# Two attention mixers: the values' products of query tiles taken in pairs

## The chip, the cores and the metric

The kernel runs on one core of a Trainium2 chip. The core has a matrix engine (TensorE, PE in the profile; its loads of the stationary operand stand in rows of their own as PEld), a vector engine (VectorE, DVE), an engine for functions and copies (ScalarE, ACT), a general one (GpSimdE, POOL) and one that issues transfers (SyncE, SP). The metric is the time of one execution on the device in microseconds. Each engine runs its own instructions in the order of its queue and waits on semaphores for the others.

## The reference, cut to what matters

Two layers work on 512 latent tokens (a grid of 8 rows by 64 columns) and 256 context tokens, 1024 channels wide, everything in 32-bit floats. A layer has three mixers: a Fourier mix, a neighbourhood attention and a latent attention. Their results are gated, merged and projected, and a gated feed-forward part follows. The context tokens read context alone, and the second layer does not renew them. The change lies in the two attentions, each with 8 heads of 64 channels:

```python
def softmax_attend(q, k, v, scale):
    s = jnp.einsum('bqhd,bkhd->bhqk', q, k, preferred_element_type=jnp.float32) * scale
    p = jax.nn.softmax(s, axis=-1).astype(v.dtype)
    return jnp.einsum('bhqk,bkhd->bqhd', p, v)
```

The latent attention lets every latent query read all 768 keys, and a context query the 256 context keys. The neighbourhood attention lets a latent query read a clamped window of 8 x 16 grid positions, with a learned bias per offset, and all 256 context keys, under one softmax:

```python
s = jnp.concatenate([s_loc.reshape(b, h, GRID_W, n_loc), s_ctx], axis=-1)
p = jax.nn.softmax(s, axis=-1).astype(v.dtype)
...
return (jnp.einsum('bhwkj,bkwjhd->bwhd', p_loc, v_win)
        + jnp.einsum('bhwc,bchd->bwhd', p_ctx, v_ctx))
```

## The kernel before

A token tile is 128 tokens: tiles 0 to 3 are latent, 4 and 5 context. Layer 0 handles six query tiles in its attentions, layer 1 only the four latent ones. Heads go in four pairs. A **unit** is one query tile of one head pair in one mixer, made by `na_unit` (neighbourhood) or `mla_unit` (latent attention), so that there are (6 + 4) x 4 x 2 = 80 units in all. A unit has four parts:

- *scores*: the products of queries and keys for both heads into PSUM banks (lines 1163 to 1167, and `mm3` at line 269), the maximum on DVE, and the exponentials on ACT. These also leave the sums of a row's probabilities in the small tile `ac`. The unnormalized probabilities are the tiles `p` and `mp`.
- *norm*: `row_scale` adds the two sums of a row (line 1041), takes reciprocals (line 1043) and spreads them to the 64 channels of each head, as the tile `rw` (line 1045), on DVE.
- *transpose*: PE turns the probabilities by key chunks of 128 into PSUM (lines 1195, 1491 and 1496), and ACT and DVE copy them into `pT` or `mpT` (lines 1198, 1492 and 1498). `scale_rows` turns `rw` in the same way (line 1051) and copies it back (line 1052).
- *values*: per key chunk and head, one f32 product with 64 channels of the values as the stationary operand and the 128 queries of the transposed probabilities as the moving one (line 1210 in the neighbourhood attention, line 1506 in the latent one). The two heads of the pair write partitions 0 to 63 and 64 to 127 of one bank, in two column halves of the array (`tile_position`). DVE multiplies by the turned scales on the way out (lines 1213 and 1509), and the last unit of a head pair issues the store to DRAM.

A latent unit of the latent attention has 6 chunks of 128 keys, which are the same for all latent tiles. A latent unit of the neighbourhood attention has the two context chunks, which are the same for all tiles, and two chunks of its own window; for tiles 0 and 3 the last of these has 64 keys. A context unit has two context chunks in both.

`pipeline` writes down the order of the units: at step n the norm of unit n-1, the scores of unit n, the values of unit n-2, and then the transposes of unit n-1. Between these steps `weave` deals out filler steps (the projections of the next head pair, gates ahead of their turn, modulation blocks) by their costs, the numbers `c` of a unit among them. Then the framework's scheduler orders the instructions of each engine with a simulated timeline and adds the waits. Tiles come from pools: `bufs` says how many buffers stand behind a tag, and a new tile waits until all users of the old one in its buffer are through. PSUM has eight banks, which all parts share through `ps()`.

The product at line 532 of the modulation blocks appears in the prediction as well: a f32 product with 256 moving columns in four column strips of 32.

Of the kernel before, what the change touches and what calls it, by code (L numbers as in the profile page):

```python
# [9 lines left out]
F32 = mybir.dt.float32  # L10
# [5 lines left out]
P = 128  # L16
# [117 lines left out]
class Kern:  # L134
# [900 lines left out]
    def row_scale(self, pool, accs, n):  # L1035

        nc = self.nc
        s = accs[:, :, 0]
        if n == 2:
            s = self.t(self.sm, [P, 2], "ssum", F32, 6)  # L1040
            nc.vector.tensor_add(s, accs[:, :, 0], accs[:, :, 1])
        r = self.t(self.sm, [P, 2], "srec", F32, 6)
        nc.vector.reciprocal(r, s)
        w = self.t(pool, [P, P], "rw", F32, 2)
        nc.vector.tensor_copy(w.rearrange("p (a b) -> p a b", a=2), r.unsqueeze(2).to_broadcast([P, 2, 64]))
        return w

    def scale_rows(self, w):

        ps = self.ps()  # L1050
        self.nc.tensor.transpose(ps[:, :P], w, self.ident)
        self.nc.scalar.copy(w, ps[:, :P])
        return w

    def qk_steps(self, l, hp):
# [32 lines left out]
        return a + b  # L1088

    def pipeline(self, groups, fills, begin=()):  # L1090

# [31 lines left out]

    def na_unit(self, l, hp, i):

# [21 lines left out]
        def scores():  # L1147
# [9 lines left out]
            st["ys"], st["p"] = self.nys, []  # L1157
            st["ac"] = self.t(self.sm, [P, 2, 2], "ac", F32, 6)
            ss = []
# [9 lines left out]
            for j in range(2):  # L1169
                s = ss[j]  # L1170
                p = self.t("na", [P, 512], "p", F32, 4)
                nm = self.t(self.sm, [P, 1], "nm", F32, 6)
                ac = st["ac"][:, j]
# [10 lines left out]
                st["p"].append(p)  # L1184

        def norm():
            st["w"] = self.row_scale("na", st["ac"], 2 if lat else 1)

        def transpose():
            ch = chunks()  # L1190
            st["pT"] = []
            for j in range(2):
                pt = self.ps()
                for c, (col, r, v) in enumerate(ch):
                    nc.tensor.transpose(pt[:r, c * P:(c + 1) * P], st["p"][j][:, col:col + r], self.ident)
                pT = self.t("na", [P, 512], "pT", F32, 4)
                full = sum(P for _, r, _ in ch if r == P)
                nc.scalar.copy(pT[:, :full], pt[:, :full])
                if full < len(ch) * P:
                    nc.scalar.copy(pT[:64, full:full + P], pt[:64, full:full + P])  # L1200
                st["pT"].append(pT)
            st["r"] = self.scale_rows(st["w"])

        def values():
            ch = chunks()
            y = self.ps()
            for c, (col, r, v) in enumerate(ch):
                for j in range(2):
                    h = 2 * hp + j
                    nc.tensor.matmul(y[64 * j:64 * j + 64, :P], v[:r, h * DH:(h + 1) * DH],  # L1210
                                     st["pT"][j][:r, c * P:(c + 1) * P], start=c == 0, stop=c == len(ch) - 1,
                                     tile_position=(0, 64 * j))
            nc.vector.tensor_mul(st["ys"][:, i * P:(i + 1) * P], y[:, :P], st["r"])
            if i == (NT if cx else NTL) - 1:
                nc.scalar.dma_start(self.ybuf[1][hp * P:(hp + 1) * P, :tt], st["ys"][:, :tt])

        f = 1.0 if lat else 0.5
        return dict(scores=scores, norm=norm, transpose=transpose, values=values, c=(0.9 * f, 0.9 * f, 1.1 * f))

    def attention(self, l):  # L1220
# [14 lines left out]
        st += self.qk_steps(l, 0)  # L1235
        units = [[self.na_unit(l, hp, i) for i in range(nq)] for hp in range(4)]
        pl = on_pool if NA_POOL else list
# [99 lines left out]
    def mla_main(self, l, steps):  # L1337
# [91 lines left out]
        self.mq = {}  # L1429
        units = [[self.mla_unit(l, hp, i) for i in range(nq)] for hp in range(4)]  # L1430
        pl = on_pool if MLA_POOL else list
# [5 lines left out]

    def mla_unit(self, l, hp, i):
        nc = self.nc
# [8 lines left out]
        def scores():  # L1448
# [3 lines left out]
            st["ys"], st["p"] = self.mys, []  # L1452
            st["ac"] = self.t(self.sm, [P, 2, 2], "ac", F32, 6)
            qq = slice(i * P, (i + 1) * P)
# [11 lines left out]
            for j in range(2):  # L1466
                scj = sc[:, 256 * j:256 * j + 256]
                p = self.t("m3", [P, T], "mp", F32, 4)
                nm = self.t(self.sm, [P, 1], "nm", F32, 6)
                ac = st["ac"][:, j]  # L1470
                if lat:
# [7 lines left out]
                st["p"].append(p)  # L1479

        def norm():
            st["w"] = self.row_scale("m3", st["ac"], 2 if lat else 1)

        def transpose():
            pT = self.t("m3", [P, 2, NT, P], "mpT", F32, 2)
            st["pT"] = pT
            if lat:
                for j in range(2):
                    pt = self.ps()
                    for c in range(4):  # L1490
                        nc.tensor.transpose(pt[:, c * P:(c + 1) * P], st["p"][j][:, c * P:(c + 1) * P], self.ident)
                    nc.scalar.copy(pT[:, j, 0:4, :], pt.rearrange("p (a b) -> p a b", b=P))
            pt = self.ps()
            for j in range(2):
                for c in range(2):
                    nc.tensor.transpose(pt[:, (2 * j + c) * P:(2 * j + c + 1) * P],
                                        st["p"][j][:, (4 + c) * P:(5 + c) * P], self.ident)
            nc.vector.tensor_copy(pT[:, :, 4:6, :], pt.rearrange("p (a c b) -> p a c b", a=2, b=P))
            st["r"] = self.scale_rows(st["w"])

        def values():
            y = self.ps()
            for a, c in enumerate(cl):
                for j in range(2):
                    h = 2 * hp + j
                    nc.tensor.matmul(y[64 * j:64 * j + 64, :P], self.vm[:, c, h * DH:(h + 1) * DH],
                                     st["pT"][:, j, c, :], start=a == 0, stop=a == len(cl) - 1,
                                     tile_position=(0, 64 * j))
            nc.vector.tensor_mul(st["ys"][:, i * P:(i + 1) * P], y[:, :P], st["r"])
# [681 lines left out]
```

## Time and profile before

| | us |
|---|---|
| median of 3 runs | 2399.32 |
| lowest and highest run | 2399.12, 2402.32 |
| profiled execution | 2407.74 |
| its span on the core | 2405.9 |
| PE busy in the span | 2292.3 |
| DVE busy | 1361.3 |
| ACT busy | 1105.7 |
| POOL busy | 991.1 |

The profile comes from one execution. "Busy" counts the time in which an engine has at least one instruction in work; matmuls overlap each other, so that a long duration of one says little and the distance between the starts of two says more. In a row of the timeline, neighbours of one kind are merged: start, time to the end of the last one, engine, line, operation, output and inputs by their names in the program, stationary shape, moving shape, count, and in brackets the idle time before it with the instruction that ended it. A row of a group has the count, the busy time in us and the mean ns of one, and then the idle time before them and what ended it. A product of f32 operands stands in the profile as two loads and two matmuls.

### The profile page before, as it was taken

What the parts mean: (1) busy time and instruction counts of PE and PEld (TensorE: products, weight loads), DVE (VectorE), ACT (ScalarE), POOL (GpSimd) and SP (SyncE); (2) the same over time, 40 slices, a digit from 0 to 9 for tenths busy, and PEclk for the clock granted to TensorE, in tenths of its full rate; (3) what the DMA queues carried; (4) which work ended last, traced back from release to release, by engine and by line L of the source; (5) the groups of instructions that cost most, each with busy time, mean ns of one, the idle gap of its engine ahead of it and who ended that gap; (6) DMA issues with size and microseconds to landing.
All of it is one profiled execution on the core that took longest, in us unless ns stands there. A gap on an engine that the chain in (4) does not pass through costs nothing. (4 is left out here: it accounts for less than half of the span.)

```text
span 2405.9 us, 37733 instructions
## 1 busy us (share of the span) xinstructions
PE 2292.3 (95%) x14370; PEld 1992.7 (83%) x14370; DVE 1361.3 (57%) x2491; ACT 1105.7 (46%) x2472; POOL 991.1 (41%) x755
## 2 busy tenths in 40 slices
PE   6999999999999998999999999999999988999997
PEld 4877688878988787999988888788888867999875
DVE  7335456658435668555541352344668566888634
ACT  4335466644332253444442252565665424555532
POOL 2311143124238446334348343324403665423483
PEclk9999999999999998999999999999999999999998
DMA  9446421117665331222252243222214642333431
GB/s 340 141 147 234 174 77 61 38 59 258 235 245 183 110 122 49 97 105 97 70 216 77 80 145 114 78 69 90 86 44 171 211 149 103 113 106 106 140 114 62
DMA packets 105409, 307.80 MB, mean 128 GB/s; under 512 B 12070, under 2 KB 21228, under 8 KB 105228
## 3 DMA queue, kind: packets, MB, share of 16 engines
q1 hardware_dynamic: 86444, 261.48, 31.8%
q10 hardware_dynamic: 15552, 38.63, 4.2%
q0 software_dynamic: 3232, 5.28, 0.8%
q8 instruction: 113, 1.85, 0.3%
q14 instruction: 68, 0.56, 0.1%
HBM read 262.06 MB, written 47.48 MB: 129 GB/s over the span
## 5 line engine op out<-in xcount | busy, mean ns | idle before, releaser
L211 POOL TENSOR_TENSOR wlo<-raw,whi 128x512 fp32r<-128x512 f32 (+2 forms) x420 | 566.1, 1356 | 889.4 <-ACT whi L210 841.5
L210 ACT CAST whi<-raw 128x512 fp32r<-128x512 f32 (+1 forms) x447 | 273.6, 616 | 431.3 <-PE ps L1648 98.5
L509 PE MATMUL ps<-tp,whi 128*128 128x384 f32 (+1 forms) x1120 | 273.7, 315 | 2.2 <-POOL tp L444 1.0
L509 PE MATMUL ps<-AH,whi 128*128 128x384 f32 (+1 forms) x636 | 197.8, 314 | 3.9 <-DVE hx L490 1.5
L509 PEld LDWEIGHTS ps<-tp,whi 128*128 128x128 f32 x1120 | 194.7, 188 | 6.7 <-issue 2.9
L509 PE MATMUL ps<-AH,wlo 128*128 128x384 f32 (+1 forms) x636 | 197.3, 311 | 1.0 <-DVE wlo L211 1.0
L277 PE MATMUL ps<-AH,whi 128*128 128x512 f32 (+1 forms) x584 | 188.1, 368 | 10.0 <-ACT hx L1890 7.4
L509 PE MATMUL ps<-AL,whi 128*128 128x384 f32 (+1 forms) x636 | 196.2, 310 | 0.0
L277 PE MATMUL ps<-AL,whi 128*128 128x512 f32 (+1 forms) x584 | 183.3, 362 | 1.5 <-DVE AL L733 1.5
L277 PE MATMUL ps<-AH,wlo 128*128 128x512 f32 (+1 forms) x584 | 183.1, 361 | 0.0
L509 PE MATMUL ps<-tp,wlo 128*128 128x384 f32 (+1 forms) x560 | 175.2, 313 | 0.0
L2003 PE MATMUL ps<-whi,hx 128*128 128x512 f32 x520 | 165.2, 397 | 8.5 <-ACT hx L1995 5.0
L325 PE MATMUL ps<-wlo,AH 128*128 128x512 f32 (+1 forms) x352 | 134.2, 382 | 0.0
L325 PE MATMUL ps<-whi,AL 128*128 128x512 f32 (+1 forms) x352 | 133.9, 381 | 0.0
L325 PE MATMUL ps<-whi,AH 128*128 128x512 f32 (+1 forms) x352 | 132.4, 384 | 0.0
L277 PEld LDWEIGHTS ps<-AH,whi 128*128 128x128 f32 x584 | 101.7, 193 | 31.9 <-ACT hx L1890 7.9
L2003 PEld LDWEIGHTS ps<-whi,hx 128*128 128x128 f32 x520 | 97.8, 189 | 33.8 <-ACT hx L1995 5.6
L509 PEld LDWEIGHTS ps<-AH,whi 128*128 128x128 f32 x636 | 119.5, 188 | 7.2 <-DVE hx L490 2.1
L509 PEld LDWEIGHTS ps<-AH,wlo 128*128 128x128 f32 x636 | 119.7, 188 | 1.4 <-DVE wlo L211 1.2
L509 PEld LDWEIGHTS ps<-AL,whi 128*128 128x128 f32 x636 | 119.6, 188 | 0.8 <-issue 0.8
L277 PEld LDWEIGHTS ps<-AL,whi 128*128 128x128 f32 x584 | 100.1, 192 | 21.4 <-DVE AL L733 2.4
L1704 POOL TENSOR_TENSOR xr<-xr,gb 128x512 f32<-128x512 f32 x80 | 114.1, 1445 | 0.4
(340 smaller groups left out, 5786.1 us busy)
## 6 DMA issues: line engine op xcount, KB each, us to landing
mraw<-in_w_mod_dram SPq DMA_DIRECT2D x80, 512.0 KB
raw<-in_w_down_dram SPq DMA_DIRECT2D x44, 512.0 KB
raw<-in_w_g_dram SPq DMA_DIRECT2D x40, 512.0 KB
raw<-in_w_gate_dram SPq DMA_DIRECT2D x36, 512.0 KB
raw<-in_w_up_dram SPq DMA_DIRECT2D x26, 512.0 KB
raw<-in_w_br_dram SPq DMA_DIRECT2D x24, 512.0 KB
gb<-th ACTq DMA_DIRECT2D x24, 384.0 KB
th<-gb SPq DMA_DIRECT2D x24, 384.0 KB
```

The costliest lines, as they stand in the source:

```text
L210: hi_eng(hi[:, :n], x)
L211: lo_eng.tensor_sub(lo[:, :n], x, hi[:, :n].bitcast(F32))
L277: self.nc.tensor.matmul(ps, w.at(wt, ws), at[:, k0 + kc, cols], start=kc == 0 and i == 0, stop=kc == nk - 1 and i == 2)
L325: self.nc.tensor.matmul(ps, a[:, k0 + kc, tok], w.at(b, ws), start=kc == 0 and i == 0, stop=kc == 2 * nb - 1 and i == 2)
L509: nc.tensor.matmul(ps, ws[0].at(wt, w), act[at], start=new and kc == 0 and i == 0, stop=kc == 3 and i == 2, skip_group_check=True)
L1704: i = op(x[:, c], x[:, c], self.gbt[g][:, c])
L2003: nc.tensor.matmul(ps, h[a][:, tok], w.at(b, ws), start=f == seq[0] and i == 0, stop=f == NF - 1 and i == 2)
```

## The change

Units 2i and 2i+1 of a head pair share a dictionary `sh`. The scores stay as they are, except that the sums of both units go into one tile `ac`. The norm of the even unit does nothing; that of the odd one treats both. The transposes stay per unit, but both write into one tile of twice the width, in which a chunk has 256 columns: 128 of the even unit and 128 of the odd one. This tile has one buffer in place of the former buffers per unit, with the same bytes in all. The turned scales are made with the odd unit, with two transposes and one copy. The values of the even unit do nothing. Those of the odd one run for both: for chunks that both units share, one product per head with 256 moving columns; for the two window chunks of the neighbourhood attention, one with 128 columns per unit, as before. One product with the scales follows for both.

The order inside the neighbourhood's values becomes: the two context chunks at 256 columns, then the window chunks of the even unit, then those of the odd one. The costs given to `weave` for the values move to the odd unit (2.0 in place of 1.1 each in the neighbourhood attention, 2.9 in place of 1.5 each in the latent one).

```diff
 def row_scale(self, pool, accs, n):
-        s = accs[:, :, 0]
+        s = accs[:, :, :, 0]
...
-        w = self.t(pool, [P, P], "rw", F32, 2)
-        nc.vector.tensor_copy(w.rearrange("p (a b) -> p a b", a=2), r.unsqueeze(2).to_broadcast([P, 2, 64]))
+        w = self.t(pool, [P, 2 * P], "rw", F32, 1)
+        nc.vector.tensor_copy(w.rearrange("p (u a b) -> p u a b", u=2, a=2), r.unsqueeze(3).to_broadcast([P, 2, 2, 64]))
         return w

 def scale_rows(self, w):
         ps = self.ps()
-        self.nc.tensor.transpose(ps[:, :P], w, self.ident)
-        self.nc.scalar.copy(w, ps[:, :P])
-        return w
+        for u in range(2):
+            self.nc.tensor.transpose(ps[:, u * P:(u + 1) * P], w[:, u * P:(u + 1) * P], self.ident)
+        self.nc.scalar.copy(w, ps[:, :2 * P])

+    def paired(self, unit, l, hp, n):
+        sh = [{} for _ in range(n // 2)]
+        return [unit(l, hp, i, sh[i // 2]) for i in range(n)]

 def na_unit(self, l, hp, i, sh):
...
         def norm():
-            st["w"] = self.row_scale("na", st["ac"], 2 if lat else 1)
+            if u == 1:
+                sh["w"] = self.row_scale("na", sh["ac"], 2 if lat else 1)

         def transpose():
             ch = chunks()
-            st["pT"] = []
+            if u == 0:
+                sh["pT"] = self.t("na", [P, 2, 4, 2 * P], "pT", F32, 1)
+            sh[u] = ch
             for j in range(2):
...
-                pT = self.t("na", [P, 512], "pT", F32, 4)
...
+                nc.scalar.copy(sh["pT"][:, j, :full, us], pt[:, :full, :])
+                if full < len(ch):
+                    nc.scalar.copy(sh["pT"][:64, j, full, us], pt[:64, full, :])
+            if u == 1:
+                self.scale_rows(sh["w"])

         def values():
+            if u == 0:
+                return
             y = self.ps()
-            for c, (col, r, v) in enumerate(ch):
+            for c in range(2):
                 for j in range(2):
...
+                    nc.tensor.matmul(y[64 * j:64 * j + 64, :2 * P], sh[1][c][2][:, h * DH:(h + 1) * DH],
+                                     sh["pT"][:, j, c, :], start=c == 0, stop=c == last, tile_position=(0, 64 * j),
+                                     skip_group_check=True)
+            for a in range(2 if lat else 0):
+                for c in range(2, 4):
+                    _, r, v = sh[a][c]
+                    for j in range(2):
+                        h = 2 * hp + j
+                        nc.tensor.matmul(y[64 * j:64 * j + 64, a * P:(a + 1) * P], v[:r, h * DH:(h + 1) * DH],
+                                         sh["pT"][:r, j, c, a * P:(a + 1) * P], start=False, stop=c == last,
+                                         tile_position=(0, 64 * j), skip_group_check=True)
-            nc.vector.tensor_mul(st["ys"][:, i * P:(i + 1) * P], y[:, :P], st["r"])
+            nc.vector.tensor_mul(st["ys"][:, (i - 1) * P:(i + 1) * P], y[:, :2 * P], sh["w"])
...
-        return dict(scores=scores, norm=norm, transpose=transpose, values=values, c=(0.9 * f, 0.9 * f, 1.1 * f))
+        return dict(scores=scores, norm=norm, transpose=transpose, values=values, c=(0.9 * f, 0.9 * f, 2.0 * f * u))

 def mla_unit(self, l, hp, i, sh):
...
         def transpose():
-            pT = self.t("m3", [P, 2, NT, P], "mpT", F32, 2)
-            st["pT"] = pT
+            if u == 0:
+                sh["pT"] = self.t("m3", [P, 2, NT, 2 * P], "mpT", F32, 1)
+            pT = sh["pT"]
...
-                    nc.scalar.copy(pT[:, j, 0:4, :], pt.rearrange("p (a b) -> p a b", b=P))
+                    nc.scalar.copy(pT[:, j, 0:4, us], pt.rearrange("p (a b) -> p a b", b=P))
...
         def values():
+            if u == 0:
+                return
             y = self.ps()
             for a, c in enumerate(cl):
                 for j in range(2):
                     h = 2 * hp + j
-                    nc.tensor.matmul(y[64 * j:64 * j + 64, :P], self.vm[:, c, h * DH:(h + 1) * DH],
-                                     st["pT"][:, j, c, :], start=a == 0, stop=a == len(cl) - 1,
+                    nc.tensor.matmul(y[64 * j:64 * j + 64, :2 * P], self.vm[:, c, h * DH:(h + 1) * DH],
+                                     sh["pT"][:, j, c, :], start=a == 0, stop=a == len(cl) - 1,
                                      tile_position=(0, 64 * j))
-        return dict(scores=scores, norm=norm, transpose=transpose, values=values, c=(1.95 * f, 1.3 * f, 1.5 * f))
+        return dict(scores=scores, norm=norm, transpose=transpose, values=values, c=(1.95 * f, 1.3 * f, 2.9 * f * u))
```

More of the change, by code (lines that the diff above doesn't have):

```diff
@@ L1037, in row_scale @@
         nc = self.nc
-        s = accs[:, :, 0]
+        s = accs[:, :, :, 0]
         if n == 2:
-            s = self.t(self.sm, [P, 2], "ssum", F32, 6)
-            nc.vector.tensor_add(s, accs[:, :, 0], accs[:, :, 1])
-        r = self.t(self.sm, [P, 2], "srec", F32, 6)
+            s = self.t(self.sm, [P, 2, 2], "ssum", F32, 4)
+            nc.vector.tensor_add(s, accs[:, :, :, 0], accs[:, :, :, 1])
+        r = self.t(self.sm, [P, 2, 2], "srec", F32, 4)
         nc.vector.reciprocal(r, s)
-        w = self.t(pool, [P, P], "rw", F32, 2)
-        nc.vector.tensor_copy(w.rearrange("p (a b) -> p a b", a=2), r.unsqueeze(2).to_broadcast([P, 2, 64]))
+        w = self.t(pool, [P, 2 * P], "rw", F32, 1)
+        nc.vector.tensor_copy(w.rearrange("p (u a b) -> p u a b", u=2, a=2), r.unsqueeze(3).to_broadcast([P, 2, 2, 64]))
         return w
@@ L1122, in pipeline, with na_unit @@
         return out
-    def na_unit(self, l, hp, i):
+    def na_unit(self, l, hp, i, sh):
         nc = self.nc
@@ L1157, in scores @@
             st["ys"], st["p"] = self.nys, []
-            st["ac"] = self.t(self.sm, [P, 2, 2], "ac", F32, 6)
+            if i % 2 == 0:
+                sh["ac"] = self.t(self.sm, [P, 2, 2, 2], "ac", F32, 4)
             ss = []
@@ L1172, in scores @@
                 nm = self.t(self.sm, [P, 1], "nm", F32, 6)
-                ac = st["ac"][:, j]
+                ac = sh["ac"][:, i % 2, j]
                 if lat:
@@ L1194, in transpose @@
                 for c, (col, r, v) in enumerate(ch):
-                    nc.tensor.transpose(pt[:r, c * P:(c + 1) * P], st["p"][j][:, col:col + r], self.ident)
-                pT = self.t("na", [P, 512], "pT", F32, 4)
[L1197 to L1201, printed above, removed]
@@ L1202, in transpose @@
-            st["r"] = self.scale_rows(st["w"])
+                    nc.tensor.transpose(pt[:r, c, :], st["p"][j][:, col:col + r], self.ident)
+                full = sum(r == P for _, r, _ in ch)
+                nc.scalar.copy(sh["pT"][:, j, :full, us], pt[:, :full, :])
[3 more added lines that the diff above has]
+                self.scale_rows(sh["w"])
         def values():
-            ch = chunks()
+            if u == 0:
+                return
@@ L1206, in values @@
             y = self.ps()
-            for c, (col, r, v) in enumerate(ch):
+            last = 3 if lat else 1
+            for c in range(2):
                 for j in range(2):
                     h = 2 * hp + j
-                    nc.tensor.matmul(y[64 * j:64 * j + 64, :P], v[:r, h * DH:(h + 1) * DH],
-                                     st["pT"][j][:r, c * P:(c + 1) * P], start=c == 0, stop=c == len(ch) - 1,
-                                     tile_position=(0, 64 * j))
-            nc.vector.tensor_mul(st["ys"][:, i * P:(i + 1) * P], y[:, :P], st["r"])
+                    nc.tensor.matmul(y[64 * j:64 * j + 64, :2 * P], sh[1][c][2][:, h * DH:(h + 1) * DH],
+                                     sh["pT"][:, j, c, :], start=c == 0, stop=c == last, tile_position=(0, 64 * j),
+                                     skip_group_check=True)
@@ L1235, in attention @@
         st += self.qk_steps(l, 0)
-        units = [[self.na_unit(l, hp, i) for i in range(nq)] for hp in range(4)]
+        units = [self.paired(self.na_unit, l, hp, nq) for hp in range(4)]
         pl = on_pool if NA_POOL else list
@@ L1429, in mla_main @@
         self.mq = {}
-        units = [[self.mla_unit(l, hp, i) for i in range(nq)] for hp in range(4)]
+        units = [self.paired(self.mla_unit, l, hp, nq) for hp in range(4)]
         pl = on_pool if MLA_POOL else list
@@ L1436, in mla_main, with mla_unit @@
         return steps
-    def mla_unit(self, l, hp, i):
+    def mla_unit(self, l, hp, i, sh):
         nc = self.nc
@@ L1452, in scores @@
             st["ys"], st["p"] = self.mys, []
-            st["ac"] = self.t(self.sm, [P, 2, 2], "ac", F32, 6)
+            if i % 2 == 0:
+                sh["ac"] = self.t(self.sm, [P, 2, 2, 2], "ac", F32, 4)
             qq = slice(i * P, (i + 1) * P)
@@ L1469, in scores @@
                 nm = self.t(self.sm, [P, 1], "nm", F32, 6)
-                ac = st["ac"][:, j]
+                ac = sh["ac"][:, i % 2, j]
                 if lat:
@@ L1479, in scores @@
                 st["p"].append(p)
+        u = i % 2
+        us = slice(u * P, (u + 1) * P)
         def norm():
-            st["w"] = self.row_scale("m3", st["ac"], 2 if lat else 1)
+            if u == 1:
+                sh["w"] = self.row_scale("m3", sh["ac"], 2 if lat else 1)
         def transpose():
-            pT = self.t("m3", [P, 2, NT, P], "mpT", F32, 2)
-            st["pT"] = pT
+            if u == 0:
+                sh["pT"] = self.t("m3", [P, 2, NT, 2 * P], "mpT", F32, 1)
+            pT = sh["pT"]
             if lat:
@@ L1497, in transpose @@
                                         st["p"][j][:, (4 + c) * P:(5 + c) * P], self.ident)
-            nc.vector.tensor_copy(pT[:, :, 4:6, :], pt.rearrange("p (a c b) -> p a c b", a=2, b=P))
-            st["r"] = self.scale_rows(st["w"])
+            nc.vector.tensor_copy(pT[:, :, 4:6, us], pt.rearrange("p (a c b) -> p a c b", a=2, b=P))
+            if u == 1:
+                self.scale_rows(sh["w"])
         def values():
+            if u == 0:
+                return
             y = self.ps()
```

6 lines of the change are left out of this document (4 added, 2 removed).

## The prediction

> **What bounds the kernel now.** I read the page first (engine totals, the chain that ended last), then busy time in windows around the four attention stages, then the tensor engine's waits there, then its timeline row by row.
>
> ```profile
> span 2405.9 us, 37733 instructions
> PE 2292.3 (95%) x14370; PEld 1992.7 (83%) x14370; DVE 1361.3 (57%) x2491; ACT 1105.7 (46%) x2472; POOL 991.1 (41%) x755
> ...
> PE 8%; DVE 4%; DMA 1%; issue 1%; ACT 0%; DVEq 0%; ACTq 0%
> ```
>
> TensorE (PE) is busy 95% of the span, nothing else over 57%. The chain is followed back only through the last 15% of the span, after all attention, so it says nothing here. The windows do (neighbourhood attention and latent attention of layer 0, then the same of layer 1; after the length each column is busy time, then the granted clock):
>
> ```profile
> core 0: us, PE busy (x) PEld busy (x) DVE busy (x) ACT busy (x) POOL busy (x), PEclk, DMA share, GB/s
> 150.00:352.00 202.00, 194.93 (x1551) 149.71 (x1549) 100.64 (x302) 110.70 (x346) 46.70 (x40) 0.98 0.46 161
> 380.00:550.00 170.00, 161.94 (x1240) 135.38 (x1241) 104.65 (x263) 94.58 (x276) 31.42 (x30) 0.97 0.15 53
> 1530.00:1668.00 138.00, 135.43 (x942) 114.01 (x940) 61.48 (x212) 91.56 (x278) 48.19 (x42) 1.00 0.26 81
> 1700.00:1830.00 130.00, 129.76 (x968) 106.17 (x967) 86.11 (x204) 81.11 (x227) 29.64 (x31) 1.00 0.25 87
> ```
>
> PE is busy 622 of 640 us, ACT at most two thirds of any window. So a microsecond taken from PE inside these windows shortens the span by nearly one; work taken from ACT or DVE shortens it by nothing. A busy PE is not yet PE at its peak, so the next view is how closely matmuls start. The products that change:
>
> ```profile
> L1506 PE MATMUL ps<-mpT,vm 128*64 128x128 f32 x832 | 64.4, 282 | 6.8 <-DVE rw L1045 6.2 <-DVE mpT L1498 0.6
> ...
> L1210 PE MATMUL ps<-pT,vc 128*64 128x128 f32 x320 | 36.8, 289 | 3.2 <-ACT pT L1198 3.2
> ```
>
> The code issues 416 products at L1506 and 160 on context chunks at L1210, half of these counts: an f32 product is two records. The durations of 282 and 289 ns are latencies that overlap; the cost is the distance between starts:
>
> ```profile
> 1741.17 0.43 PE L1506 MATMUL ps<-mpT,vm 128*64 128x128 f32 x2
> 1741.53 0.50 PE L277 MATMUL ps<-AL,whi 128*128 128x512 f32 x1
> ...
> 1747.94 0.39 PE L269 MATMUL ps<-mkh,mql 96*128 96x512 f32 x1
> 1748.17 0.39 PE L269 MATMUL ps<-mkl,mqh 96*128 96x512 f32 x1
> 1748.49 1.53 PE L1506 MATMUL ps<-mpT,vm 128*64 128x128 f32 x24
> 1749.95 1.09 PE L1491 MATMUL ps<-ident,mp 128*128 128x128 f32 x8
> ...
> 1753.62 0.43 PE L1506 MATMUL ps<-mpT,vm 128*64 128x128 f32 x2
> 1753.99 1.09 PE L1491 MATMUL ps<-ident,mp 128*128 128x128 f32 x8
> 1755.01 1.52 PE L1506 MATMUL ps<-mpT,vm 128*64 128x128 f32 x22
> 1756.46 0.66 PE L1496 MATMUL ps<-ident,mp 128*128 128x128 f32 x4
> 1756.96 0.27 PE L1051 MATMUL ps<-ident,rw 128*128 128x128 f32 x1
> 1756.99 0.48 PE L277 MATMUL ps<-CH,whi 128*128 128x512 f32 x1
> ```
>
> The two heads of a unit sit in the two column halves of the array and run side by side, so 24 records are 12 slots. A unit comes whole (x24: 1.46 us to the next start) or split: one head's first product alone (x2 at 1741.17, 0.36 us, two slots), other work, then the rest (x22 at 1755.01, 1.45 us: the other head alone for two slots, then ten shared). 1.45 - 0.36 us over ten slots is **109 ns a slot**; what is left of 0.36 is 0.14 us at the edge of each stretch. Going in costs too: the 512-column product ahead takes 0.32 us to the next start (1748.17 to 1748.49) against 0.23 (1747.94 to 1748.17). An **edge is 0.14 + 0.09 = 0.23 us**. A split costs another edge and two slots, 0.23 + 0.22 = 0.45 us.
>
> **The change, part by part.**
>
> *Streaming.* The same kind of f32 product with 256 moving columns, four column strips side by side, is in the trace:
>
> ```profile
> 213.56 1.93 PE L532 MATMUL ps<-mraw,sT 128*32 128x256 f32 x32
> 215.43 0.66 PE L1195 MATMUL ps<-ident,p 128*128 128x128 f32 x4
> ```
>
> 32 records are 8 slots: (1.87 - 0.14)/8 = 0.216 us, against 2 x 0.109 = 0.218. Width is paid column for column; halving instructions and weight loads saves 2 ns a wide slot. 576 shared products are 576 narrow slots and become 288 wide ones: **0.6 us**. The nearest rows bound it by 0 and by 0.03 us a slot (the smallest distance above, 1756.96 to 1756.99), 8.6 us; I take the 256-column row, which is the same operation.
>
> The Trainium skill, TensorEngine Tiling (Array Packing), section Instruction Overhead, gives every matmul some 60 cycles of overhead. At its 2.4 GHz that is an estimate of 25 ns, or 7.2 us for 288 slots; the row of 0.216 us speaks against it for this width.
>
> *Edges.* This is where the gain lies. Counting stretches of L1210 and L1506 in the whole PE timeline gives 126 for the 80 units (10 tiles x 4 head pairs x 2 mixers); 45 of them are an x2 piece. The first and the last:
>
> ```profile
> 188.28 0.66 PE L1210 MATMUL ps<-pT,vc 128*64 128x128 f32 x8
> ...
> 1823.48 1.52 PE L1506 MATMUL ps<-mpT,vm 128*64 128x128 f32 x22
> ```
>
> Now: 80 x 0.23 = 18.4 us of edges, 45 x 0.45 = 20.3 us of splits. After: 40 blocks, 9.2 us of edges. A block waits for the same copies of its second unit as a unit does now, so I let the share of split blocks stay at 45/80: 22.5, each at 0.23 + 2 x 0.216 = 0.66 us, 14.9 us. Gain 38.7 - 24.1 = **14.6 us**. The share of splits is the unknown: none gives 38.7 - 9.2 = 29.5 us, all 40 give 38.7 - 9.2 - 26.4 = 3.1 us. I stay between because nothing in the release of a block's first product changes.
>
> *Chunks of 64 rows.* In neighbourhood attention, tiles 0 and 3 end on a chunk of 64 rows.
>
> ```profile
> 202.72 0.66 PE L1210 MATMUL ps<-pT,vc 128*64 128x128 f32 x8
> 203.21 0.75 PE L1210 MATMUL ps<-pT,vl 128*64 128x128 f32 x8
> 203.89 0.66 PE L1195 MATMUL ps<-ident,p 128*128 128x128 f32 x4
> ```
>
> 8 slots take 1.17 us against 8 x 0.109 + 0.14 = 1.01: the change of height costs 0.15 us. In the first pair that chunk is now followed by tile 1's full ones, a second change: 8 blocks x 0.15 = **-1.2 us**. At the least it is nothing (if the first change is merely brought forward), at the most twice that.
>
> *Scales.* Both scale transposes now go with the second unit. PE has the same 80, and each still stands behind other transposes (1756.46, 1756.96): no change; if one were torn loose, 0.03 to 0.11 us. DVE and ACT lose work off the path:
>
> ```profile
> L1492 ACT COPY mpT<-ps 128x512 f32<-128x512 f32 x64 | 36.1, 597 | 21.1 <-PE ps L1491 18.4 <-DVE rw L1045 1.5 <-DVE srec L1043 1.0
> ...
> L1052 ACT COPY rw<-ps 128x128 f32<-128x128 f32 x80 | 22.5, 281 | 14.9 <-PE ps L1051 14.6
> ```
>
> ACT loses 40 of the 80 copies at L1052, at most 40 x 0.28 = 11 us. On DVE go 40 small sums, reciprocals and fixed parts of spreads and products. PE's work in these windows hides all of it: 0. The transposed copies go to strided columns in the same amount; a price per byte would hide the same way.
>
> *The ends of the stages.* The product of the last unit but one now runs after the last unit's copies.
>
> ```profile
> 349.80 0.93 PE L1210 MATMUL ps<-pT,vc 128*64 128x128 f32 x8 [1.71 <-ACT pT L1198]
> 353.16 0.90 PE L1291 MATMUL ps<-ident,cq 128*128 128x128 f32 x3 [2.44 <-DVE cq L1323]
> ```
>
> Behind the neighbourhood stage PE waits for DVE's cq anyhow, which hides it; the end of layer 1's latent stage is filled with gate products. All four exposed would be four such blocks, 0.6 to 1.5 us each, some 4 us; none, 0. I take **-1.0 us**.
>
> *Order and buffers.* The values' cost moves to odd units, so filler work is dealt differently; between a unit's scores and its transposes there is still exactly one values block. The tile of transposed probabilities goes from one per unit with a spare to a single one per pair. I take 0; the price if wrong is rival 2.
>
> **Sum**: 14.6 + 0.6 - 1.2 - 1.0 = 13.0 us off the profiled execution's 2407.7 (its span 2405.9 and 1.8 around it), so 2394.7. That execution lies 8.4 us above the median of the runs, 2399.3, from which the same step leads to **2386 us**.
>
> **Rivals.**
> 1. *More blocks are torn.* A paired block needs more copies before it can run through, and every one of the 40 is split. Gain 3.1 + 0.6 - 1.2 - 1.0 = 1.5 us: 2398, no change that can be told. For it: 45 of 80 are split now; against: a unit's copies come as early as before.
> 2. *The single buffer stalls (slower).* Copies of the next pair's first unit must wait for the whole block of the pair before, and ACT's following exponentials stand behind them in its queue; PE then waits for probabilities to transpose. For it: at 1753.99 transposes run ahead of the rest of a unit's products, so their copies now use the spare. If PE loses one copy's time per pair (597 ns), 40 x 0.60 = 24 us: 2386 + 24 = 2410. It outweighs the gain from 13/40 = 0.33 us a pair. Against: ACT is busy 81 of 130 us in the fullest PE window, about 3 us free a unit, more than the 2.6 us (12 x 0.216) of a paired block.
> 3. *No block is torn*, as its first unit is ready a step early: 29.5 + 0.6 - 2.2 = 28 us, 2371. For it: whole units occur (x24 at 1748.49); against: it is always the second head that is late, and that stays.
> 4. *Every removed slot carries a fixed cost* of 0.03 us: 8.6 instead of 0.6, 2378. Against it stand the two rows of 0.109 and 0.216. The overhead that the Trainium skill states (above) is of this kind.
>
> **How the numbers follow.** Forecast 0.45, rival 1 0.24, rival 2 0.13, rival 3 0.13, rival 4 0.05. The range from 2371 to 2404 takes in all but rival 2 and the worst of rival 1; the forecast's own is 2380 to 2393. A measurement of this kernel tells about 0.2%, 4.8 us, from no change: faster is the forecast and rivals 3 and 4, 0.62 with one in a hundred taken off; same 0.23; slower 0.15.
>
> **What would show it.** Right: 576 records fewer at the two values lines, wide slots of 0.216 us; some 60 to 65 stretches in place of 126; PE's waits in the windows as small as now. Wrong: wide slots far under 0.216 (rival 4 or more); most blocks torn with an x2 piece of 0.57 us (rival 1); waits of PE on ACT's exponentials, or ACT idle on PE ahead of its copies to the transposed tile (rival 2). Waits that grow at a stage's end would show that I priced the ends too low.

## The result, and the profile after

| | before | after |
|---|---|---|
| median of 6 runs, us | 2401.14 | 2387.43 |
| lowest and highest run, us | 2399.12, 2407.73 | 2384.53, 2394.93 |
| profiled execution, us | 2407.74 | 2387.02 |

The ratio after to before is 0.9947, with a 95% interval of 0.9928 to 0.9966: between 8 and 17 us of 2400 are saved, around 12.7. The forecast of 2386 is 1.4 us below the median, and 2387.43 lies in its own range of 2380 to 2393. One execution of the kernel before, beside the first four experiments below, took 5695.72 us and stands in no ratio.

From the page of the kernel after, the span and the engine totals:

```profile
span 2385.2 us, 36359 instructions
...
PE 2272.1 (95%) x13794; PEld 1971.4 (83%) x13794; DVE 1331.3 (56%) x2339; ACT 1101.7 (46%) x2432; POOL 992.4 (42%) x755
```

PE has 13794 records in place of 14370, the 576 fewer that were forecast. It stays the bound. The groups of the kernel after by line and shape (count, busy us, mean ns, then idle time before them) show where they went:

```profile
L1538 PE MATMUL ps<-mpT,vm 128*64 128x256 f32 x416 | 51.7, 390 | 2.2 <-DVE mpT L1526 2.2
L1224 PE MATMUL ps<-pT,vc 128*64 128x256 f32 x160 | 29.3, 396 | 3.1 <-ACT pT L1210 2.8 <-DVE kl L1080 0.3
```

832 and 320 narrow records have become 416 and 160 wide ones.

The busy time by stage, with bounds at the same point of the work in both kernels: neighbourhood and latent attention of layer 0, then of layer 1. The columns are those of the prediction's windows; first before, then after.

```profile
core 0: us, PE busy (x) PEld busy (x) DVE busy (x) ACT busy (x) POOL busy (x), PEclk, DMA share, GB/s
156.80:383.30 226.50, 219.64 (x1671) 169.91 (x1671) 125.50 (x345) 129.06 (x380) 63.44 (x54) 0.97 0.43 151
383.30:564.80 181.50, 174.21 (x1312) 146.55 (x1313) 116.00 (x273) 100.40 (x283) 43.12 (x37) 0.97 0.19 66
1535.00:1704.70 169.70, 164.86 (x1062) 137.68 (x1061) 83.38 (x253) 112.53 (x322) 69.03 (x63) 0.98 0.26 84
1704.70:1837.40 132.70, 132.46 (x975) 108.22 (x974) 90.38 (x205) 83.21 (x224) 33.52 (x34) 1.00 0.25 90
```

```profile
157.20:380.30 223.10, 216.57 (x1576) 166.42 (x1576) 115.99 (x299) 127.40 (x368) 59.62 (x54) 0.97 0.44 153
380.30:551.60 171.30, 165.03 (x1088) 134.70 (x1089) 112.34 (x230) 99.31 (x271) 42.15 (x37) 0.98 0.20 69
1519.50:1691.00 171.50, 162.22 (x999) 134.28 (x998) 80.64 (x218) 111.16 (x312) 68.38 (x63) 0.98 0.26 84
1691.00:1817.70 126.70, 125.52 (x782) 99.80 (x781) 85.73 (x178) 82.78 (x219) 33.90 (x35) 1.00 0.27 95
```

The four lengths add up to 710.4 us before and 692.6 after, 17.8 less; PE's busy time falls from 691.2 to 669.3, by 21.8. So the stages were shortened by 4 us less than PE's busy time. Layer 1's neighbourhood stage got longer, 169.7 to 171.5, although PE is busy 2.6 us less in it. A length from one profile is good to some 3 us (with the latent attention alone paired, below, this stage has its old units and takes 172.9 and 171.4), so the waits say more. PE's waits in that window (us in total, times, longest), before and then after:

```profile
PE ps L1291 <- DVE cq L1323: 2.4, 1, 2.4
PE ps L1195 <- ACT p L1179: 1.3, 2, 1.0
PE ps L277 <- ACT CH L1299: 0.7, 1, 0.7
PE ps L1051 <- DVE rw L1045: 0.3, 1, 0.3
```

```profile
PE ps L1313 <- DVE cq L1345: 3.5, 1, 3.5
PE ps L1208 <- ACT p L1186: 2.1, 3, 1.0
PE ps L1053 <- DVE rw L1046: 1.6, 3, 0.6
PE ps L277 <- ACT CH L1321: 1.1, 1, 1.1
PE ps L1224 <- ACT pT L1210: 0.8, 1, 0.8
```

They grow from 4.7 to 9.1 us. Over all four stages they grow from 21.0 to 24.8.

The two profiled executions differ by 20.7 us, more than the medians. One wait explains most of the surplus, PE's for the reloaded results of the mixers in the merge, over the whole kernel, before and after:

```profile
PE ps L1648 <- DVE yl L1599: 16.4, 2, 10.0
```

```profile
PE ps L1680 <- DVE yl L1631: 5.6, 1, 5.6
```

The second, 10 us wait in layer 1 made that stage 79.9 us in place of 73.7, from the first of its products to the last. A wait of 9 to 10 us stands there in the profiles of five of the nine kernels below that have pairs and of none of the three without, but of the kernel before too and not of the kernel after, so it isn't tied to the change. Without these 6.2 us the profiles differ by 14.5, close to the 13.7 between the medians.

### The profile page after: what moved, and what is told of

It reads as the page before. It is cut to its first block, busy times and chain, and to the rows that moved or that the text cites. A ratio compares the mean times of both kernels' runs of the same rounds, so it can differ in the third digit from the quotient of the medians.

```text
span 2385.2 us, 36359 instructions
## 1 busy us (share of the span) xinstructions
PE 2272.1 (95%) x13794; PEld 1971.4 (83%) x13794; DVE 1331.3 (56%) x2339; ACT 1101.7 (46%) x2432; POOL 992.4 (42%) x755
```

## The experiments

The theory: PE's time at the edges of stretches of values' products is what the change saves, since a pair needs one stretch in place of two and fewer are torn; part of it is lost again where a stage ends. The rivals: the width itself (rival 4 of the prediction), a stall by the single buffer (rival 2), the merged scales, and the order in which the two heads' products are issued. Times are medians; each ratio is to the kernel before, timed beside it, with its 95% interval. The kernel before did not take the same time beside each (2405.42, 2401.21 and 2399.85 us in the three groups in which the kernels were timed), so compare kernels by their ratios. "Attentions" is the length of the four stages together in the one profile of that kernel (before 710.4, after 692.6); an unchanged repeat can be judged by the kernel with fewer buffers below, 711.4.

**Pairs, but at 128 columns.** The kernel after, with each shared chunk as two products of 128 columns per head, back to back (the same in the latent attention):

```diff
-                for j in range(2):
-                    nc.tensor.matmul(y[64 * j:64 * j + 64, :2 * P], ..., sh["pT"][:, j, c, :], ...)
+                for q in range(2):
+                    for j in range(2):
+                        nc.tensor.matmul(y[64 * j:64 * j + 64, q * P:(q + 1) * P], ...,
+                                         sh["pT"][:, j, c, q * P:(q + 1) * P], start=c == 0 and q == 0, ...)
```

> The paired kernel, but each shared chunk is multiplied as two products of 128 columns per head, one for each unit, right behind one another: as many products and weight loads as the kernel before, in blocks for two units as in the changed one. The planned order has 58 stretches of values products (before 126, changed 57). Theory of the edges (what is saved is entering and leaving the two-column arrangement, 0.23 us each, and lone-head pieces): the time stays at the changed kernel's, within 3 us of 2387, ratio to before 0.994. Rival, loads and width (the gain comes from half as many products and loads, 0.03 us each): most of the gain goes, 2395 to 2401, ratio 0.998 to 1.000. On the trace: slots of 0.109 us, about twice as many as the wide ones of 0.216.

Measured: 2383.27 us, ratio 0.9915 (0.9891 to 0.9939), attentions 686.7. From its page and its groups:

```profile
PE 2271.6 (95%) x14370; PEld 1997.0 (84%) x14370; DVE 1340.0 (56%) x2339; ACT 1103.5 (46%) x2432; POOL 987.5 (41%) x755
...
L1540 PE MATMUL ps<-mpT,vm 128*64 128x128 f32 x832 | 51.4, 276 | 1.6 <-DVE mpT L1527 1.6
```

All 14370 records are back, and PE is busy as long as with the wide products (2271.6 against 2272.1 us). The group's busy time is even 51.4 us, where it was 64.4 before and 51.7 after. The width of 256 columns is worth nothing that can be measured; the pairing carries the gain. Rival 4 falls: its 8.6 us would have brought the ratio to about 0.998, above the interval. So does, for products that stand back to back and read as time added to each, the overhead per matmul that the prediction took from the Trainium skill, TensorEngine Tiling (Array Packing), section Instruction Overhead. Why the attentions are another 5.9 us shorter here than after (692.6) isn't known.

**No pairs, but the late head first.** The kernel before, with the two heads' products issued in the other order in both values loops:

```diff
-                for j in range(2):
+                for j in (1, 0):
```

> The kernel before, unpaired, with one edit: the two heads' products of a chunk are issued second head first. The planned order then has 92 stretches in place of 126 and no piece with one head alone (45 before). Theory of the edges: 34 edges at 0.23 us and 45 pieces at two slots of 0.109 us less, 7.8 + 9.8 = 17.6 us, about 2383.5 us, ratio 0.9927, as good as the pairing or better. Rival, loads and width: nothing of that kind is changed, ratio 1.000. Rival, work taken from ACT and DVE: nothing taken, ratio 1.000.

Measured: 2390.09 us, 0.9944 (0.9922 to 0.9966), attentions 700.9; some 13 us saved. A torn latent unit of layer 1 in the timeline of the kernel before, then the first and the third unit of that stage in this one, which are whole:

```profile
1722.27 0.43 PE L1506 MATMUL ps<-mpT,vm 128*64 128x128 f32 x2
...
1724.23 1.52 PE L1506 MATMUL ps<-mpT,vm 128*64 128x128 f32 x22
```

```profile
1704.30 1.53 PE L1506 MATMUL ps<-mpT,vm 128*64 128x128 f32 x24
...
1722.61 1.53 PE L1506 MATMUL ps<-mpT,vm 128*64 128x128 f32 x24
```

Of 126 stretches 92 are left, and no lone first product. With the prediction's prices that is 34 x 0.23 + 45 x 0.22 = 17.7 us; the ratio gives 13.4. Two edited lines that change no product, no copy and no byte bring as much as the whole pairing. The edges are real, though a part of what they free is lost again: PE's wait for `cq` at the end of layer 1's neighbourhood stage, 2.4 us before, is 4.5 us here.

**Pairs and the late head first.** The same edit in the kernel after.

> The changed kernel with the second head's product of each shared chunk first. The planned order has 46 stretches in place of 57, and 3 pieces with one head alone in place of 13. Theory of the edges: 11 x 0.23 + 10 x 0.43 = 6.8 us under the changed kernel, about 2380.5, ratio 0.9915. If the ends of the stages and not PE set what is left: no more than 2 us under it, ratio 0.994. Rival, loads and width: the changed kernel's time, ratio 0.9945.

Measured: 2389.13 us, 0.9941 (0.9918 to 0.9964), attentions 692.5: nothing more that can be told, where the edges alone would have given 6.8 us. The stretches fall from 57 to 46, and over the whole kernel PE's busy time falls from 2272.1 to 2263.8 us, but its waits in the attentions rise from 24.8 to some 31. Layer 1's neighbourhood stage, with the columns of the windows above:

```profile
1517.70:1687.10 169.40, 158.09 (x990) 132.52 (x989) 81.67 (x216) 110.43 (x309) 68.80 (x63) 0.97 0.25 82
```

PE is busy 158.1 us there, 4.1 less than after. Some 2 us of that are nine projection products of 512 columns that stand in the next stage here; and its waits rise from 9.1 to 11.1 us. Work taken off PE in this stage no longer shortens the stage by as much.

**Scales per unit again.** The kernel after, with sums, reciprocals, spreads, transposes, their copies and the products with the scales done once per unit:

```diff
-        w = self.t(pool, [P, 2 * P], "rw", F32, 1)
-        nc.vector.tensor_copy(...)
+        for u in range(2):
+...
+            nc.vector.tensor_copy(w[:, u * P:(u + 1) * P]..., r.unsqueeze(2).to_broadcast([P, 2, 64]))
```

> The changed kernel, but the scales are made per unit again: two sums, two reciprocals, two spreads, two copies back and two products of 128 columns per pair in place of one each; all at the odd unit. The planned order has 54 stretches and 11 lone-head pieces. Theory that PE hides this work: the changed kernel's time, 2384 to 2389, ratio 0.993 to 0.995. Rival, part of the gain comes from work taken from ACT and DVE (40 copies of 0.28 us on ACT, 40 x (0.18 + 0.16 + 0.29) us on DVE): 2395 or more, ratio 0.997 and up.

Measured: 2385.75 us, 0.9928 (0.9902 to 0.9954), attentions 691.5. The 40 copies and the 40 groups of small DVE instructions that come back cost no time that can be measured: the merged scales are worth nothing, as the prediction said.

**One mixer paired, the other as before.** The unpaired unit function and its helpers are those of the kernel before, and its units are made one by one. To fit, the unpaired units' small tiles (`ac`, `ssum`, `srec`) had 3, 2 and 2 buffers under tags of their own.

```diff
-        units = [self.paired(self.na_unit, l, hp, nq) for hp in range(4)]
+        units = [[self.na_unit(l, hp, i) for i in range(nq)] for hp in range(4)]
```

> Only the latent attention is paired; the neighbourhood attention is as before, with its scales per unit. The planned order has 64 + 26 = 90 stretches; 2 lone-head pieces in the latent part in place of 21. Theory that the edges count and that the neighbourhood stages lose theirs in waits at their ends: 36 x 0.23 + 21 x 0.22 - 2 x 0.43 = 12.0 us, nearly the whole gain of the changed kernel, ratio 0.9945 to 0.9955. Rival, both mixers give their share of the edges: less than two thirds of the changed kernel's gain, ratio 0.997.

> Only the neighbourhood attention is paired; the latent attention is as before. The planned order has 32 + 62 = 94 stretches and 12 wide lone-head pieces in place of 24 narrow ones. By the edges alone 32 x 0.23 + 24 x 0.22 - 12 x 0.43 = 7.5 us, ratio 0.997. Theory that the ends eat it (PE comes to the end earlier and waits there for the vector and scalar engines): 0 to 3 us, ratio 0.9985 to 1.000, with the second neighbourhood stage no shorter than before and PE's waits in it longer by 3 to 5 us.

Measured: latent attention alone 2398.37 us, 0.9983 (0.997 to 0.9997), attentions 697.5; neighbourhood alone 2411.87 us, 1.004 (1.0025 to 1.0056), attentions 708.6. Both miss what was expected, the second on the other side. The buffers of the small tiles were a second edit, so both were made again with four buffers each, as many as in the kernel after, under shared tags (the kernel before has six):

```diff
-            s = self.t(self.sm, [P, 2], "ssum1", F32, 2)
+            s = self.t(self.sm, [P, 2], "ssum", F32, 4)
...
-            st["ac1"] = self.t(self.sm, [P, 2, 2], "ac1", F32, 3)
+            st["ac1"] = self.t(self.sm, [P, 2, 2], "ac", F32, 4)
```

> Latent attention alone paired, as in latent_only, with one difference: the tiles of the row sums and reciprocals have four buffers each, as in the changed kernel, in place of the two or three to which they were cut there for space. The two runs of one mixer alone did not add up: their attention stages were 12.8 and 1.7 us shorter than before in the profiles (17.8 with both), their times 4 us less and 10 us more. If the few small buffers cost it: now 12 us less than before, ratio 0.995. If the stages outside the attentions shift by themselves from kernel to kernel: attention stages again 11 to 14 us shorter, the time anywhere from 0.992 to 1.000.

> The same for the neighbourhood attention alone, four buffers each for the small tiles. If the few small buffers cost it: 0 to 3 us less than before, ratio 0.9985 to 1.000. If the rest shifts by itself: attention stages again 0 to 4 us shorter, the time anywhere from 0.996 to 1.005.

Measured: latent alone 2390.59 us, 0.9959 (0.9944 to 0.9974), attentions 695.6; neighbourhood alone 2405.02 us, 1.0014 (1.0005 to 1.0024), attentions 709.1. Both medians fell by some 6 us against the kernel before, but that the buffers did it isn't shown. The profiled executions of each couple lie only 1.4 and 0.5 us apart (2400.14 and 2398.73, 2405.89 and 2405.38), and the executions of one kernel by far more (2384.9 to 2402.1 for the first latent one, 2384.3 to 2399.7 for the second): how many of them have the merge's wait of 10 us, which both latent profiles have, can move a median as well. What follows, by one profile each: in the attentions themselves the latent mixer has nearly all of the gain (710.4 - 695.6 = 14.8 us, the neighbourhood mixer 1.3; together 16.1 against 17.8 measured for both). Why the neighbourhood pairing alone makes the kernel slower stays open. Its gate products behind layer 0's attentions took 142 us in the profile where the kernel before has 136; but the kernel with pairs at 128 columns has 144 there and is not slower.

**The gates last.** The end of the neighbourhood stage weaves gate products (`G[3]`) among the projections for the latent attention (`c_steps`, whose result is `cq`). In the kernel after, these projections now come first and the gates behind them:

```diff
-        st += self.pipeline(units, fill + [([], swap + weave(pl(c_steps), G[3]))])
+        st += self.pipeline(units, fill + [([], swap + pl(c_steps) + G[3])])
```

> The changed kernel with one edit: at the last head pair of the neighbourhood attention the gate that is made ahead of its turn (one in layer 1, none in layer 0) is dealt out after the latent attention's input projection and not between its steps. Its products then stand in PE's queue where PE waited 3.5 us for the normalized projection (cq). Theory of the ends: layer 1's neighbourhood stage gets 3 to 4 us shorter and that wait is under 1 us, about 2384 us, ratio 0.993. Rival, PE's wait is a symptom and the chain through ACT and DVE takes as long wherever the products stand: no change, ratio 0.9945.

Measured: 2380.40 us, 0.9921 (0.9908 to 0.9934), attentions 685.3. Layer 1's neighbourhood stage and PE's waits in it:

```profile
1518.40:1684.60 166.20, 160.73 (x1000) 133.46 (x999) 80.96 (x218) 111.32 (x312) 69.58 (x63) 0.99 0.26 86
```

```profile
PE ps L1208 <- ACT p L1186: 2.1, 3, 1.0
PE ps L1053 <- DVE rw L1046: 2.0, 3, 1.1
PE ps L277 <- ACT CH L1321: 1.1, 1, 1.1
```

The stage is 166.2 us long in place of 171.5, and the wait for `cq` of 3.5 us is gone. Of the 5.3 us, 3.9 are PE's waits; the rest is its busy time for the same work, at a granted clock of 0.99 in place of 0.98. The loss at the end of this stage is shown, and it can be had back. For the whole kernel the two intervals still overlap (0.9908 to 0.9934 here, 0.9928 to 0.9966 without this edit).

**Both small edits in the kernel after** (heads swapped and gates last).

> Both edits on the changed kernel: second head first (46 stretches in the planned order, 3 lone-head pieces) and the gate after the projection. Theory of the edges and the ends together: 6.8 + 3.5 us under the changed kernel, about 2377, ratio 0.990. If what swapping saves is lost again in waits elsewhere, as it was without the gate's move: 2384, ratio 0.993.

Measured: 2378.51 us, 0.9909 (0.9895 to 0.9923), attentions 683.0, 46 stretches. The interval lies just below that of the change alone (0.9928 to 0.9966): of the versions here it is the fastest, ahead of both kernels, though not to be told from the gates alone or from the pairs at 128 columns.

**Fewer buffers in the kernel before.**

```diff
-                pT = self.t("na", [P, 512], "pT", F32, 4)
+                pT = self.t("na", [P, 512], "pT", F32, 2)
...
-            pT = self.t("m3", [P, 2, NT, P], "mpT", F32, 2)
+            pT = self.t("m3", [P, 2, NT, P], "mpT", F32, 1)
```

> The kernel before, with half the buffers for the transposed probabilities: two half-unit tiles in place of four in the neighbourhood attention, one in place of two in the latent one, so that a unit's copies wait for the values products of the unit before it. The planned order has 65 + 62 stretches (64 + 62 before). Theory that the single buffer is harmless: within 3 us of before, ratio 0.999 to 1.001, attention stages within 3 us of 710. Rival, the single buffer stalls: one copy of 0.6 us for each of 80 units on PE, 48 us, ratio 1.02; a quarter of that is still 1.005.

Measured: 2400.56 us, 1.0003 (0.999 to 1.0016), attentions 711.4. In the unpaired kernel, where the copies of the next unit must wait for the products of the one before, a single buffer costs nothing that can be measured. The reverse, two buffers for the paired tile, wasn't run.

**Both small edits in the kernel before.** Is the pairing needed at all?

> The kernel before, unpaired, with both small edits: second head first, and the gate after the latent attention's input projection. The planned order has 93 stretches and no lone-head piece. Theory of the edges and the ends: 17.6 us less the part lost in the neighbourhood stages, which was 13.5 us with swapping alone, and 3 to 5 us more by the gate, about 2384, ratio 0.9925; the pairing then has some 93 - 46 = 47 edges, 10 us, left to give over it at the most.

Measured: 2386.52 us, 0.9938 (0.992 to 0.9957), attentions 694.4. Three edited lines without any pairing give what the change gives (0.9947). On top of them pairing adds the step from 0.9938 to 0.9909, some 7 us; the two intervals overlap by a little (0.992 to 0.9923), while the attentions fall from 694.4 to 683.0.

## Why the prediction was right, point by point

**Streaming: right.** A whole latent block in the timeline of the kernel after:

```profile
1707.69 0.39 PE L269 MATMUL ps<-mkh,mql 96*128 96x512 f32 x1
1707.92 0.39 PE L269 MATMUL ps<-mkl,mqh 96*128 96x512 f32 x1
1708.24 2.81 PE L1538 MATMUL ps<-mpT,vm 128*64 128x256 f32 x24
1710.98 1.09 PE L1519 MATMUL ps<-ident,mp 128*128 128x128 f32 x8
```

2.74 us are 12 x 0.216 + 0.14 but for 0.01, and the entry is again 0.32 us (1707.92 to 1708.24) where two 512-column products stand 0.23 apart (1707.69 to 1707.92). The prices of a wide slot and of the two parts of an edge that the prediction counted hold to the hundredth.

**Edges: right in kind, undersized.** The price of a torn block was right: 0.57 us from the lone first product to the next instruction.

```profile
1646.30 0.65 PE L1224 MATMUL ps<-pT,vc 128*64 128x256 f32 x2
1646.87 0.46 PE L325 MATMUL ps<-wlo,AH 128*128 128x416 f32 x1
...
1647.26 0.86 PE L1224 MATMUL ps<-pT,vc 128*64 128x256 f32 x5
```

Their number was not. I let "the share of split blocks stay at 45/80: 22.5"; it fell to 13 of 40 lone products, and to 57 stretches where 62.5 were forecast. The step that failed is that one share was taken for both mixers. In the neighbourhood attention the share stayed the same, 24 of 40 units and then 12 of 20 blocks; in the latent attention it went from 21 of 40 to 1 of 20. Why the latent blocks stay whole isn't shown. The first and the last of the 57:

```profile
193.37 0.62 PE L1224 MATMUL ps<-pT,vc 128*64 128x256 f32 x2 [0.30 <-DVE kl L1080]
...
1799.20 2.80 PE L1538 MATMUL ps<-mpT,vm 128*64 128x256 f32 x22
```

With the prediction's prices, 0.23 us per stretch and two slots per lone product, the counts by stage give:

| stage | stretches | lone products | by these, us | length, us | PE's waits, us |
|---|---|---|---|---|---|
| neighbourhood, layer 0 | 38 to 20 | 14 to 8 | -3.8 | -3.4 | 8.1 to 8.4 |
| latent, layer 0 | 36 to 16 | 11 to 0 | -7.0 | -10.2 | 8.0 to 6.2 |
| neighbourhood, layer 1 | 26 to 12 | 10 to 4 | -3.7 | +1.8 | 4.7 to 9.1 |
| latent, layer 1 | 26 to 9 | 10 to 1 | -5.7 | -6.0 | 0.2 to 1.1 |
| all | 126 to 57 | 45 to 13 | -20.2 | -17.8 | 21.0 to 24.8 |

So the edges gave 20.2 us where 14.6 were forecast, inside the bounds of 3.1 to 29.5. The first and the last row come out within 0.4 us. The second gains 3.2 us more than its count, 1.8 of them fewer waits; the third loses 5.5 us, 4.4 of them more waits.

The price of an edge is itself a little short. Eight transposes right behind a stretch take 1.09 us to the end of the last (1710.98 above, and 1749.95 and 1753.99 in the prediction); behind a full-width product of the kernel before they take 1.04:

```profile
1725.68 0.50 PE L277 MATMUL ps<-AL,whi 128*128 128x512 f32 x1
1726.02 1.04 PE L1491 MATMUL ps<-ident,mp 128*128 128x128 f32 x8
```

So the first one behind a stretch loses another 0.05 us, which the prediction's 0.14 + 0.09 leaves out. For 69 stretches that is an estimate of 3.5 us more, if it holds behind every one.

**The ends of the stages: undersized.** The forecast was -1.0 us, at most some -4. Layer 1's neighbourhood stage alone lost 5.5 us against its count. Its end after, and the end of layer 0's:

```profile
1651.35 0.28 PE L325 MATMUL ps<-whi,AL 128*128 128x160 f32 x1
1655.16 0.52 PE L1313 MATMUL ps<-ident,cq 128*128 128x128 f32 x3 [3.54 <-DVE cq L1345]
```

```profile
344.82 0.65 PE L1224 MATMUL ps<-pT,vc 128*64 128x256 f32 x2
346.94 1.08 PE L1224 MATMUL ps<-pT,vc 128*64 128x256 f32 x6 [1.47 <-ACT pT L1210]
351.23 0.90 PE L1313 MATMUL ps<-ident,cq 128*128 128x128 f32 x3 [3.21 <-DVE cq L1345]
```

In layer 1 the gate products run out at 1651.35, and PE then stands for 3.54 us until DVE has written `cq`; before it was 2.4. In layer 0 the last block is torn with nothing left to put between its parts, and the two waits are 4.68 us where they were 1.71 + 2.44. The prediction priced an exposed end as one block (0.6 to 1.5 us) and took PE's wait for `cq` as cover ("PE waits for DVE's cq anyhow, which hides it"); it is not cover but the thing that grew. That the order of gates and projections decides it is shown by the run with the gates last, in which the wait is gone and 5.3 us came back in that stage; that PE reaches it earlier because it has less to do is argued, though the kernel before with its heads swapped, which saves PE's time without pairs, has a longer wait there too (4.5 us). The waits grew as the prediction's last paragraph said they would if the ends were priced too low.

**The sum.** With these sizes it is 20.2 + 0.6 - 1.2 - 5.5 = 14.1 us, where 13.0 was forecast and the medians differ by 13.7: the edges' +5.6 and the ends' -4.5 cancel, and that the forecast is nearer than its terms is luck. The attentions' 17.8 holds 3.7 us more than this sum, about what the estimate of the longer edge gives. Outside them, the merge's wait apart, 3.3 us were lost (1695.5 - 6.2 to 1692.6). The place is behind the merge of layer 1: from there to the end of the span PE does the same 2598 records in 436.6 us before and 442.7 after, busy 400.8 and 404.6 of them. The cause stays open, and it may be no more than what two executions differ by.

**Changes of height: right.** The first blocks of layer 1 in the timeline after:

```profile
1559.77 1.08 PE L1224 MATMUL ps<-pT,vc 128*64 128x256 f32 x8
1560.69 1.19 PE L1232 MATMUL ps<-pT,vl 128*64 128x128 f32 x16
1561.81 1.09 PE L1208 MATMUL ps<-ident,p 128*128 128x128 f32 x8
...
1566.95 1.08 PE L1224 MATMUL ps<-pT,vc 128*64 128x256 f32 x8
1567.86 1.34 PE L1232 MATMUL ps<-pT,vl 128*64 128x128 f32 x16
1569.14 0.87 PE L1208 MATMUL ps<-ident,p 128*128 128x128 f32 x6
```

Whole blocks are of two lengths, 2.04 and 2.19 us. 4 x 0.216 + 8 x 0.109 + 0.14 are 1.88, so that the one has a change of 0.16 and the other a second one of 0.15.

**Scales: right**, by the run with the scales per unit. **Order and buffers: right** so far as the run with fewer buffers goes: rival 2 shows nowhere, neither as a stall in the windows after nor in the kernel before with half the buffers.

**Rivals 1 and 3** (all blocks torn, none torn) are answered by the count of 13 in 40. The prediction's reason for rival 3, "its first unit is ready a step early", may be what kept most latent blocks whole, but no run tests it.

Left open: whether the small tiles' buffers cost anything, why the neighbourhood pairing alone is slower outside the attentions, and why PE's waits grow by so much with pairing and swapping together that they save no more than either.

## What to carry to other kernels

Where short matmuls in one tile shape stand between matmuls in another, count the stretches and price their edges from the distances between starts, before counting instructions or columns. Try the other order where two products share a stretch: two edited lines here were worth as much as a restructured pair. The reading behind it, that the scheduler's timeline has the second head's operand late, is inferred from the effect. And when PE gets faster, look at what it reaches at the end of the stage: order the filler so that work which somebody waits for goes first, and work that nobody waits for is left for the end.

## What was not expected of the hardware and its schedule

A torn unit looked like a late copy; this one isn't one on the chip. Around the lone product at 1741.17 of the kernel before, which the prediction quotes, ACT and then DVE did:

```profile
1737.69 1.31 ACT L1492 COPY mpT<-ps 128x512 f32<-128x512 f32 x2
```

```profile
1739.03 0.68 DVE L1498 COPY mpT<-ps 128x512 f32<-128x512 f32 x1
```

All copies of the unit's probabilities had ended by 1739.71, 1.5 us ahead, and yet six full-width products, from 1741.53 on, stand ahead of the second part at 1743.13. PE runs its queue in the order in which the scheduler wrote it down, so the piece was torn off when the kernel was built; swapping the heads in the source removes all 45.

The edge of 0.23 us per stretch is the price of going from full-width products to column halves and back. The Trainium skill, TensorEngine Tiling (Array Packing), section Key Properties, says that a change of tiling mode drains the engine; the trace agrees in that each change costs time, 0.09 us going in and 0.14 us going out.

And the reload of the mixers' results in layer 1's merge either fits or makes PE wait another 9 to 10 us: the stage takes 73.7 us in the profile after, 79.9 before, 80.6 with the gates last. Whichever falls into the profiled execution moves that stage by as much as half of this change. That it varies from one execution to the next of the same kernel is likely, not shown: each kernel has one profile, and four of the six with the wait are the slowest execution of their kernel or the one but slowest.
